# One scores tile for a chunk, weight parts loaded two entries ahead, half the norm products, the sinks' exponential last

## The chip, the cores and the metric

The kernel runs on one core of one Trainium2 chip. It is one launch. The metric is the device time of that launch in microseconds, as the median of several runs. Beside it one execution was taken by the hardware profiler; its views are what the prediction argues from.

## What is computed

One decoder block on 2048 positions of width 1024, all in float32. Cut to the part that the change touches:

```python
q = partial_rope(rmsnorm(q, q_norm), positions) * scale     # 16 query heads of 64
k = partial_rope(rmsnorm(k, k_norm), positions)             # 2 key heads
s = q @ k.T over the block before and the own block, window 128, else -inf
m = maximum(max(s), sink)
p = exp(s - m);  denom = sum(p) + exp(sink - m)
out = (p / denom) @ v
x = x + (sigmoid(gate_pool) * pooled + sigmoid(gate_attn) * out) @ w_out
x = x + (silu(gate) * val) @ w_down                          # after a causal convolution of width 3
```

Ahead of it stand one projection of the normed input into pooling channels, queries, keys, values and two gates, and a pooling mixer with four windows.

## The kernel before

The sequence is worked in two chunks of 1024 positions, one after the other. A chunk runs through the same stages: `mixer` (keys and values, queries, attention, pooling, gates), `out_proj`, `up` and the class `Down`. The change touches `mixer` alone. A product in float32 is made as three products of rounded halves (`mm3`, L235), so every projection of 128 channels by 512 positions (`project`) is 24 matmuls into one PSUM bank. Two such banks exist (tag `f`), two of tag `a`, two of tag `t`, and one double bank of tag `s`.

**Keys stage.** For each of the 8 blocks of 128 positions, `raw` makes 24 matmuls of 256 columns into a bank `a`, `block_a` and `block_b` norm and rotate the keys, and `turn` transposes them (L714). Between the blocks stand fillers: in the first chunk the folding of two weight matrices (`fold`) and the query projections of own = 1; in the second chunk the query projections alone.

**Query projections.** `queries(c, j, n, ...)` projects the 128 channels j of 8 (j // 4 is `own`, a half of the 16 heads) for the half n of the chunk's positions. For the norm of each head the squares of the 4 projections of one `own` are summed over the head's channels. Before, a pair of projections (j even, then j odd) had an accumulator of its own from the pool `qp` (tag `Q`, 6 buffers of 2 KB a partition): ACT squares the even one into it (L736), squares the odd one into a second Q tile (L739), DVE adds the two (L740), and TensorE multiplies the sum with `heads8`, a 0/1 matrix, in 4 matmuls of 8 columns (L753). The trace shows each of these as two records of a matmul and two of a weight load. DVE adds the first pair's result to e1 (L756) and the second pair's to that (L759), and GpSimd raises it to -0.5 (L761). The rotated, split queries go to DRAM (`qd`) and come back one block at a time.

**Attention.** `mixer` walks over 32 items per chunk: 4 groups of 4 heads, 8 blocks each. An item's `scores` makes 8 matmuls of 256 columns (L797; at a chunk's start L799 and L802) into the double bank `s`, of which there is one. DVE masks them (L806), takes the maximum (L811), makes the exponent's bias (L812, L813) and the sinks' exponent (L814). ACT makes the exponential of the sinks (L815) and of the scores, one instruction per head (L818) with the sum over a row, and DVE divides (L820 to L822). `probabilities`, one item later, transposes them (L829), splits them (L831, L832) and masks them on GpSimd (L835); `values`, two items later, multiplies with the values (L854). One or two projections (queries, gates, pooling channels) stand behind each item as fillers.

**Weights.** The class `Stream` hands out weights in a fixed list of entries. When entry i is taken, the loads up to i + 2 are issued and the parts (the rounded halves) up to i + 2 are made. In the first chunk a part is made by ACT and DVE from a loaded tile, and written to DRAM. In the second chunk a part is not made but loaded back from there (`made`, 1 MB each) into one of the 19 buffers of pool `up` (tag `U`), and the load is issued at the time at which the part would have been made.

**Order.** The program is written in one order, and a scheduler puts each engine's instructions into an order of its own when the program is built: an instruction comes when the scheduler takes its inputs and its buffer to be ready. So an edit in one place shifts the order on all engines around it. The engines then work their lists strictly in order, and every load and store stands in the one list of SP.

Of the kernel before, what the change touches and what calls it, by code (L numbers as in the profile page):

```python
# [16 lines left out]
F32 = mybir.dt.float32  # L17
F32R = mybir.dt.float32r
I32 = mybir.dt.int32
U8 = mybir.dt.uint8  # L20
AF = mybir.ActivationFunctionType
ALU = mybir.AluOpType
# [4 lines left out]
P = 128  # L27
# [48 lines left out]
class Stream:  # L76
# [27 lines left out]
            self.loaded += 1  # L104

    def part(self, n):
        while self.parted < min(n, len(self.entries)):
            self.tiles[self.parted] = self.split(self.entries[self.parted],
                                                 self.raws.pop(self.parted))
            self.parted += 1  # L110
# [81 lines left out]
def block_kernel(ctx: ExitStack, tc: tile.TileContext, x, xT, pos, vec, qkn, w_poolT, w_pool, w_q, w_kv,  # L192
                 w_gp, w_ga, w_out, w_up, w_down, outT):
    nc = tc.nc
    V, G, A = nc.vector, nc.gpsimd, nc.scalar
# [6 lines left out]
    up_ = pool("up", 19)  # L202
    fp = pool("fp", 4)
    mp = pool("mp", 5)
    qp = pool("qp", 6)
    sp = pool("sp", 2)
    ps = pool("ps", 2, space=PSUM)
    ps2 = pool("ps2", 1, space=PSUM)
# [19 lines left out]
    between = []  # L228
# [158 lines left out]
    raw = [rp.tile([P, 8, P], F32, "R") for _ in range(3)] + [mp.tile([P, 8, P], F32, "M")]  # L387
# [242 lines left out]
    def project(hs, w, n, tag="f"):  # L630

        c = slice(n * 512, (n + 1) * 512)
        out = ps.tile([P, 512], F32, tag)
        mm3(out, [(w[:, 0, k, :], w[:, 1, k, :], hs[k][:, 0, c], hs[k][:, 1, c])
                  for k in range(KT)])
        if between:
            between.pop()()
        return out, c
# [88 lines left out]
    def queries(c, j, n, hs, ta, st):  # L727
        if n == 0:
            st["q", j] = stream.get("q", j, later=later)
        pq, c_ = project(hs, st["q", j], n)  # L730
        if j % 2 == 0:
            st["raw"] = mp.tile([P, 2, 512], F32, "M"), qp.tile([P, 512], F32, "Q")
        raw, acc = st["raw"]
        A.copy(raw[:, j % 2], pq)
        if j % 2 == 0:
            A.square(acc, pq)  # L736
            return
        sq = qp.tile([P, 512], F32, "Q")
        A.square(sq, pq)  # L739
        V.tensor_add(acc, acc, sq)  # L740
        parts = up_.tile([P, 2, 2, 512], F32R, "U")
        if j % 4 == 1:
            rotate(raw, st["rows"], c_, parts[:, 0].bitcast(F32))
        A.copy(parts[:, 0], raw)
        V.tensor_sub(parts[:, 1], raw, parts[:, 0].bitcast(F32))
        own, at = j // 4, j % 4
        for i in range(2):
            for e, r in enumerate(STARTS[at - 1 + i]):
                load(qd[own][n][:, r:r + 8].rearrange("a d h t -> (d h) a t"),
                     parts[64 * e:64 * e + 64, :, i].bitcast(F32))  # L750
        pn = ps.tile([P, 512], F32, "t")[:, 0:32].rearrange("p (b h) -> p b h", b=4)
        for b in range(4):
            nc.tensor.matmul(pn[:, b], acc[:, b * P:(b + 1) * P], heads8, start=True, stop=True)  # L753
        r = rq[:, own, 4 * n:4 * n + 4]
        if at == 1:
            V.tensor_tensor(r, pn, e1[:, c, 4 * n:4 * n + 4].unsqueeze(2)  # L756
                            .to_broadcast([P, 4, 8]), op=ALU.add)
        else:
            V.tensor_add(r, pn, r)  # L759
            r = r.rearrange("p b h -> p (b h)")  # L760
            G.tensor_tensor(r, r, mhalf, op=ALU.pow)  # L761

    def rotate(x, rows, c_, t):

# [20 lines left out]
    def scores(it):  # L785
        c, q4, n, g, qT = it["c"], it["q4"], it["n"], it["q4"] // 2, it["qT"]
        b = c * NB + n
        kt = it["kts"][g]
        sc = ps2.tile([P, 4, 256], F32, "s")
        if b == 0:  # L790
            V.memset(sc[:, :, 0:P], -1e30)
        for h in range(4):
            st = qT[:, h, :]
            for a in range(2):
                fl = dict(start=(a == 0), stop=(a == 1))
                if n > 0:
                    nc.tensor.matmul(sc[:, h, :], st, kt[:, a, (n - 1) * P:(n + 1) * P], **fl)  # L797
                else:
                    nc.tensor.matmul(sc[:, h, P:256], st, kt[:, a, 0:P], **fl)  # L799
            if n == 0 and b > 0:  # L800
                for a in range(2):
                    nc.tensor.matmul(sc[:, h, 0:P], st, it["carry"][:, a], start=(a == 0),  # L802
                                     stop=(a == 1))


        V.copy_predicated(sc[:, :, 0:P], causal.unsqueeze(1).to_broadcast([P, 4, P]),  # L806
                          sc[:, :, P:256])
        sk = slice(4 * q4, 4 * q4 + 4)
        st = sp.tile([P, 6, 4], F32, "st")
        mx, nm, es, rs, dn = (st[:, i] for i in range(5))  # L810
        V.reduce_max(mx, sc[:, :, 0:P], axis=AX.X)  # L811
        V.scalar_tensor_tensor(nm, mx, -1.0, it["rq"], op0=ALU.mult, op1=ALU.mult)  # L812
        V.tensor_tensor(nm, nm, nsink[:, sk], op=ALU.min)  # L813
        V.tensor_sub(es, nm, nsink[:, sk])  # L814
        A.activation(es, es, AF.Exp)  # L815
        pr = qp.tile([P, 4, P], F32, "Q")
        for h in range(4):
            A.activation(pr[:, h, :], sc[:, h, 0:P], AF.Exp, bias=nm[:, h:h + 1],  # L818
                         scale=it["rq"][:, h:h + 1], accum_out=rs[:, h:h + 1])
        V.tensor_add(dn, rs, es)  # L820
        V.reciprocal(dn, dn)
        V.tensor_tensor(pr, pr, dn.unsqueeze(2).to_broadcast([P, 4, P]), op=ALU.mult)  # L822
        it["pr"] = pr
# [554 lines left out]
    def mixer(c, hs, kvw):  # L1378
        kts, vs, raw, block_a, block_b, turn = keys_values(c, hs, kvw)
        ta, st = {}, {}  # L1380
        if c > 0:
            st["rows"] = rope_rows(c)
        for n in range(NB):
            if c == 0 and n == 2:
                st["rows"] = rope_rows(c)
            if c == 0 and n == 0:
                load_rest()
            if c == 0 and n == 1:
                make_h(0, 1, hs)
            if c == 0 and n == 3:  # L1390
                make_h(0, 2, hs)
                for i in range(4, NB):
                    squares(0, i, row(0, i))
            pk = [raw(0), raw(1)] if n == 0 else pk[1:] + ([raw(n + 1)] if n + 1 < NB else [])
            fills = list(first_fillers(c)[n])
            if c == 0 and n == 0:
                for i in range(4):
                    squares(0, i, rows[i])
            if c == 0 and n % 4 == 0:
                norm1(0, n, n + 4)  # L1400
                spread(r1[:, 0, n:n + 4], n * P)
            block_a(n, pk[0])
            block_b(n)
            if n == 2 and c == 0:
                turn(0)
            for f in fills:
                filler(*f, c, hs, ta, st)
            if n > 1 or n == c == 1:
                turn(n - 1)
            run_later()  # L1410
        turn(NB - 1)
        keep_weights(("kv",), kvw)
        items = [dict(c=c, q4=q4, n=n, kts=kts, vs=vs, ta=ta)
                 for q4 in (3, 2, 1, 0) for n in range(NB)]
        for it in items[0:2]:
            load_queries(it)
        for i in range(len(items)):
            group, n = divmod(i, NB)
            scores(items[i])
            if i + 2 < len(items):  # L1420
                load_queries(items[i + 2])
            if i > 1:
                values(items[i - 2])
            run_later()
            fills = fillers(c, group)[n]
            if i > 0 and len(fills) == 1:
# [24 lines left out]
        return ms + [mixed(ta, 0)]  # L1451
# [89 lines left out]
```

## Time and profile before

| | us |
|---|---|
| median of 3 runs | 2463.49 |
| lowest and highest of them | 2461.58, 2464.21 |
| the profiled execution | 2459.19 |
| span in its trace | 2456.9 |
| TensorE busy in the span | 2421.4 |
| VectorE (DVE), ScalarE (ACT) busy | 1876.9, 1124.8 |

The profiled execution's own time is 2.3 us longer than the span of its trace, and 4.3 us below the median. In the views PE stands for TensorE's matmuls, PEld for its weight loads, SP for the queue of the transfers. "L753 PE MATMUL t<-heads,Q" is a matmul of source line 753 into a tile of tag t from the tiles heads8 and Q. In a view of idle time "<- DVE Q L740" names the instruction whose end let the engine go on. In the view of waits the numbers are the microseconds in total, how often, and the longest. The first chunk's mixer stage ends at about 520 us, the second chunk's runs from 1240 to about 1730 us.

### The profile page before, as it was taken

What the parts mean: (1) busy time and instruction counts of PE and PEld (TensorE: products, weight loads), DVE (VectorE), ACT (ScalarE), POOL (GpSimd) and SP (SyncE); (2) the same over time, 40 slices, a digit from 0 to 9 for tenths busy, and PEclk for the clock granted to TensorE, in tenths of its full rate; (3) what the DMA queues carried; (4) which work ended last, traced back from release to release, by engine and by line L of the source; (5) the groups of instructions that cost most, each with busy time, mean ns of one, the idle gap of its engine ahead of it and who ended that gap; (6) DMA issues with size and microseconds to landing.
All of it is one profiled execution on the core that took longest, in us unless ns stands there. A gap on an engine that the chain in (4) does not pass through costs nothing.

```text
span 2456.9 us, 30720 instructions
## 1 busy us (share of the span) xinstructions
PE 2421.4 (99%) x11398; PEld 2010.8 (82%) x11398; DVE 1876.9 (76%) x3028; ACT 1124.8 (46%) x2150; POOL 146.5 (6%) x101
## 2 busy tenths in 40 slices
PE   9999999999999999999999999999999999999999
PEld 8877888887888888788888788888888888887887
DVE  8687887766988878899845767665569888788994
ACT  7445444444555555543522433333445554554432
POOL 0113111100000000000002211110000000000000
PEclk9999999999999999999999999999999999999999
DMA  9664452368222233644333542131553222228321
GB/s 338 224 197 133 172 180 110 109 220 296 97 77 86 94 112 108 211 164 143 132 125 124 166 146 100 57 125 48 184 172 103 77 87 90 82 69 283 131 75 52
DMA packets 139029, 337.88 MB, mean 138 GB/s; under 512 B 12288, under 2 KB 48640, under 8 KB 127872
## 3 DMA queue, kind: packets, MB, share of 16 engines
q1 hardware_dynamic: 138880, 335.92, 40.1%
q8 instruction: 90, 1.47, 0.2%
q14 instruction: 59, 0.48, 0.1%
HBM read 231.67 MB, written 104.20 MB: 137 GB/s over the span
## 4 chain that ended last, share of the span: by engine, by line
PE 87%; DVE 8%; ACT 2%; DMA 1%; issue 1%; POOL 0%; SPq 0%; DVEq 0%; ACTq 0%; POOLq 0%
PE f L235 31%; PE f L1069 18%; PE t L1069 10%; PE a L1069 4%; PE a L1359 4%; PE f L1359 4%; PE s L1359 4%; PE t L1359 4%; PE s L797 2%; PE a L854 2%; PE a L235 2%; DVE F L906 1%; ACT Q L818 1%; PE t L829 1%; PE t L753 1%
## 5 line engine op out<-in xcount | busy, mean ns | idle before, releaser
L235 PE MATMUL f<-U,U 128*128 128x512 f32 (+1 forms) x3936 | 918.8, 389 | 7.9 <-DVE U L219 3.7
L235 PEld LDWEIGHTS f<-U,U 128*128 128x128 f32 x3936 | 725.4, 188 | 158.3 <-DVE U L219 7.2
L1069 PE MATMUL f<-U,U 128*128 128x512 f32 x1512 | 359.7, 389 | 1.3 <-ACT Q L1087 1.3
L1069 PEld LDWEIGHTS f<-U,U 128*128 128x128 f32 x1512 | 283.3, 188 | 61.6 <-ACT Q L1087 2.2
L1135 DVE SCALAR_TENSOR_TENSOR M<-F,vc,M 128x1024 f32<-128x1024 f32 x176 | 225.0, 1282 | 127.9 <-ACT M L1132 127.5
L1069 PE MATMUL t<-U,U 128*128 128x512 f32 x1080 | 254.5, 389 | 0.3 <-ACT Q L1087 0.3
L1069 PEld LDWEIGHTS t<-U,U 128*128 128x128 f32 x1080 | 202.5, 188 | 43.2 <-ACT Q L1087 1.1
L818 ACT ACTIVATE Q<-s,st,rq 128x128 f32<-128x128 f32 x256 | 114.2, 453 | 139.6 <-DVE st L813 123.4
L331 ACT CAST U<-R 128x1024 fp32r<-128x1024 f32 x120 | 125.4, 1053 | 65.7 <-DVE R L352 34.0
L332 DVE TENSOR_TENSOR U<-R,U 128x1024 fp32r<-128x1024 f32 x120 | 146.7, 1222 | 0.0
L1069 PE MATMUL a<-U,U 128*128 128x512 f32 x576 | 138.6, 389 | 0.0
L1069 PEld LDWEIGHTS a<-U,U 128*128 128x128 f32 x576 | 108.0, 188 | 22.3
L1069 PE MATMUL f<-U,M 128*128 128x512 f32 x504 | 122.3, 390 | 4.0 <-DVE F L1113 4.0
L1318 ACT CAST U<-U 128x1024 fp32r<-128x1024 f32 x74 | 77.0, 1050 | 87.3 <-PE a L1359 26.8
L835 POOL TENSOR_SCALAR_AFFINE_SELECT M<-M 128x1024 fp32r<-128x1024 f32 x64 | 81.8, 1279 | 579.0 <-DVE M L832 331.4
L1069 PEld LDWEIGHTS f<-U,M 128*128 128x128 f32 x504 | 94.4, 188 | 24.4 <-DVE F L1113 4.9
L1132 ACT ACTIVATE M<-F,vc 128x1024 f32<-128x1024 f32 x88 | 109.3, 1243 | 1.3
L1121 ACT COPY F<-f 128x512 f32<-128x512 f32 x42 | 24.7, 587 | 178.3 <-PE f L1069 178.3
L219 DVE TENSOR_TENSOR U<-R,U 128x512 fp32r<-128x512 f32 x142 | 93.6, 691 | 7.2 <-ACT U L218 5.9
L1319 DVE TENSOR_TENSOR U<-U,U 128x1024 fp32r<-128x1024 f32 x74 | 89.7, 1221 | 11.0 <-ACT U L1318 11.0
L218 ACT CAST U<-R 128x512 fp32r<-128x512 f32 x142 | 80.6, 617 | 20.4 <-DMA R<-w_ga 5.1
L1318 ACT CAST F<-U 128x1024 fp32r<-128x1024 f32 x46 | 48.3, 1050 | 88.2 <-PE a L1359 52.3
(269 smaller groups left out, 3669.2 us busy)
## 6 DMA issues: line engine op xcount, KB each, us to landing
R<-w_up SPq DMA_DIRECT2D x80, 512.0 KB, 3.7
actd<-M SPq DMA_DIRECT2D x44, 512.0 KB, 2.6
U<-w_down SPq DMA_DIRECT2D x88, 256.0 KB, 5.3
U<-actd SPq DMA_DIRECT2D x88, 256.0 KB, 5.4
qd<-U SPq DMA_DIRECT2D x64, 256.0 KB, 3.7
Q<-qd SPq DMA_DIRECT2D x64, 256.0 KB, 3.8
R<-w_out SPq DMA_DIRECT2D x32, 512.0 KB, 5.1
U<-kept SPq DMA_DIRECT2D x12, 1024.0 KB, 7.5
```

The source lines that it names most:

```text
L219: last = V.tensor_sub(lo[:, t], src[:, t], hi[:, t].bitcast(F32))
L235: nc.tensor.matmul(out, a, b, start=(i == 0), stop=(i == n - 1))
L331: A.copy(t[:, 0], raw)
L332: V.tensor_sub(t[:, 1], raw, t[:, 0].bitcast(F32))
L818: A.activation(pr[:, h, :], sc[:, h, 0:P], AF.Exp, bias=nm[:, h:h + 1], scale=it["rq"][:, h:h + 1], accum_out=rs[:, h:h + 1])
L835: G.affine_select(own.rearrange("p a h q -> p (a h) q"), pa.bitcast(F32).rearrange("p a h q -> p (a h) q"), pattern=[[0, 8], [1, P]], base ...
L1069: nc.tensor.matmul(bank, a[:, x, k, :], b[k // 2][:, y, k % 2, :], start=(first and i == 0), stop=(i == 11), skip_group_check=True)
L1132: A.activation(y, u[:, 2:], AF.Identity, bias=cw[:, 3, m:m + 1], scale=cw[:, 2, m:m + 1])
L1135: V.scalar_tensor_tensor(y, u[:, j:j + T], cw[:, j, m:m + 1], y, op0=ALU.mult, op1=ALU.add)
L1318: A.copy(hi, src)
L1319: V.tensor_sub(lo, src, hi.bitcast(F32))
L1359: nc.tensor.matmul(into[m], u[:, 0, c_], v[:, 1], start=(first and j == 0), stop=(k == n - 1 and j == 2), skip_group_check=True)
```

## The change

It has four parts, all within `mixer` and the weight stream.

1. The double bank `s` is taken once for all 32 items of a chunk, where each item took it anew.
2. Where the entry taken last but one is a gate or a pooling weight and the part to come is one that lies in DRAM already (second chunk), its load is issued one entry earlier.
3. The squares of all 4 projections of an `own` go into one accumulator, so 4 matmuls with `heads8` per `own` and half remain of 8, and one addition per pair more is made on DVE (3 additions of 128x512 where there were 2). The squares go into tiles that exist already (the raw tile's second half, or the parts' tile) in place of a Q tile. The matmuls stand in the list `between`, from which the next projection takes them behind its own 24.
4. In `scores` the sinks' exponent and exponential (L814, L815) are written behind the four exponentials of the scores.

```diff
     def part(self, n):
+        if self.used > 0 and self.entries[self.used - 1][0] in ("ga", "pu", "pg"):
+            n += n in self.raws and self.raws[n] is None
         while self.parted < min(n, len(self.entries)):
...
+        own, at = j // 4, j % 4
+        if at == 0:
+            st["acc", n] = qp.tile([P, 512], F32, "Q")
+        acc = st["acc", n]
         if j % 2 == 0:
-            st["raw"] = mp.tile([P, 2, 512], F32, "M"), qp.tile([P, 512], F32, "Q")
-        raw, acc = st["raw"]
+            st["raw"] = mp.tile([P, 2, 512], F32, "M")
+        raw = st["raw"]
         A.copy(raw[:, j % 2], pq)
-        if j % 2 == 0:
+        if at == 0:
             A.square(acc, pq)
             return
-        sq = qp.tile([P, 512], F32, "Q")
+        if at == 2:
+            A.square(raw[:, 1], pq)
+            V.tensor_add(acc, acc, raw[:, 1])
+            return
+        parts = up_.tile([P, 2, 2, 512], F32R, "U")
+        sq = parts[:, 1, 0].bitcast(F32)
         A.square(sq, pq)
         V.tensor_add(acc, acc, sq)
-        parts = up_.tile([P, 2, 2, 512], F32R, "U")
...
+        if at == 3:
+            between.append(lambda: query_norms(c, own, n, acc))
+
+    def query_norms(c, own, n, acc):
         pn = ps.tile([P, 512], F32, "t")[:, 0:32].rearrange("p (b h) -> p b h", b=4)
         for b in range(4):
             nc.tensor.matmul(pn[:, b], acc[:, b * P:(b + 1) * P], heads8, start=True, stop=True)
...
-        sc = ps2.tile([P, 4, 256], F32, "s")
+        if n == 0 and q4 == 3:
+            it["bank"]["s"] = ps2.tile([P, 4, 256], F32, "s")
+        sc = it["bank"]["s"]
...
-        V.tensor_sub(es, nm, nsink[:, sk])
-        A.activation(es, es, AF.Exp)
         pr = qp.tile([P, 4, P], F32, "Q")
         for h in range(4):
             A.activation(pr[:, h, :], sc[:, h, 0:P], AF.Exp, bias=nm[:, h:h + 1],
                          scale=it["rq"][:, h:h + 1], accum_out=rs[:, h:h + 1])
+        V.tensor_sub(es, nm, nsink[:, sk])
+        A.activation(es, es, AF.Exp)
```

What it moves is seen in the built programs; lines of the changed kernel have numbers that are 3 to 15 higher (`mm3` is L238, the norm matmul L768, the transposition of keys L717, the exponentials L831 and L834, the splits of weights L222).

On TensorE, in the keys stage of the second chunk, before: the end of a key block (bank a_10656) with the norm matmuls of a query pair in it, and the next projection's begin (f_10707).

```order
L235 MATMUL a_10656<-U_10419,U_10309 128x256 x3
L235 MATMUL a_10656<-U_10419,U_10326 128x256 x3
L753 MATMUL t_10641<-heads_6_179,Q_10543 128x8 x4
L714 MATMUL t_10647<-identr_91,Q_10512 128x128 x4
L235 MATMUL a_10656<-U_10419,U_10345 128x256 x3
L235 MATMUL a_10656<-U_10419,U_10364 128x256 x3
L235 MATMUL f_10707<-U_10219,U_10421 128x512 x3
```

The same stage in the changed program, at the first norm matmuls that it has there: the last of the 24 matmuls of one projection (f_11007), and the next one (f_11076).

```order
L238 MATMUL f_11007<-U_10282,U_10584 128x512 x3
L238 MATMUL f_11007<-U_10301,U_10584 128x512 x3
L768 MATMUL t_11032<-heads_6_179,Q_10479 128x8 x4
L717 MATMUL t_11043<-identr_91,Q_10907 128x128 x4
L238 MATMUL f_11076<-U_10156,U_10859 128x512 x3
```

The norm matmuls of the first pair are gone, those that remain stand behind a whole projection that follows the one whose squares they sum, and there are 8 groups of them in the program where there were 16.

On ScalarE, at an item of the first chunk, before: the exponentials of the scores (L818, s_3414) with that of the sinks (L815) among them.

```order
L929 ACTIVATE F_3306<-f_3387,vc_145 128x512
L818 ACTIVATE Q_3430,st_3424<-s_3414,st_3424,rq_229 128x128 x2
L815 ACTIVATE st_3424<-st_3424 128x4
L818 ACTIVATE Q_3430,st_3424<-s_3414,st_3424,rq_229 128x128 x2
L864 COPY Q_3445<-a_3440 64x256
```

And in the changed program, at an item of the same group.

```order
L846 CAST M_3904<-t_3899 128x512
L831 ACTIVATE Q_3867,st_3863<-s_1598,st_3863,rq_229 128x128 x4
L834 ACTIVATE st_3863<-st_3863 128x4
L879 COPY Q_3884<-a_3879 64x256 x2
L900 ACTIVATE F_3913<-f_3914,vc_145 128x512
```

Before, the sinks' exponential stood within the four exponentials in 63 of the 64 items; now it stands behind them in all.

On VectorE, in the keys stage of the first chunk, before: the split of a fold's weights (L219, into U_898 and M_903) and the rotation and squares of the second query projection (L769, L770, L740).

```order
L770 SCALAR_TENSOR_TENSOR M_830<-M_830,vc_145,U_688 64x512
L219 TENSOR_TENSOR U_898<-R_794,U_898 128x512 x2
L219 TENSOR_TENSOR M_903<-R_796,M_903 128x256 x2
L691 TENSOR_TENSOR Q_969<-vf_218 128x2x64
L769 SCALAR_TENSOR_TENSOR U_872<-M_830,vc_145,U_688 64x512
L740 TENSOR_TENSOR Q_831<-Q_831,Q_869 128x512
```

And in the changed program, the rotation (L781 to L784), the addition of the squares (L752) and the same split (L222, U_891).

```order
L781 SCALAR_TENSOR_TENSOR U_869<-M_831,vc_145,U_688 64x512
L752 TENSOR_TENSOR Q_830<-Q_830,U_869 128x512
L782 SCALAR_TENSOR_TENSOR M_831<-M_831,vc_145,U_688 64x512
L783 TENSOR_TENSOR M_831<-M_831,U_869 64x512
L784 TENSOR_TENSOR M_831<-M_831,U_869 64x512
L222 TENSOR_TENSOR U_891<-R_794,U_891 128x512 x2
```

The split of the fold's weights has moved from ahead of the second projection's rotation to behind it.

More of the change, by code (lines that the diff above doesn't have):

```diff
@@ L730, in queries @@
         pq, c_ = project(hs, st["q", j], n)
+        own, at = j // 4, j % 4
+        if at == 0:
+            st["acc", n] = qp.tile([P, 512], F32, "Q")
+        acc = st["acc", n]
         if j % 2 == 0:
-            st["raw"] = mp.tile([P, 2, 512], F32, "M"), qp.tile([P, 512], F32, "Q")
-        raw, acc = st["raw"]
+            st["raw"] = mp.tile([P, 2, 512], F32, "M")
+        raw = st["raw"]
         A.copy(raw[:, j % 2], pq)
-        if j % 2 == 0:
+        if at == 0:
             A.square(acc, pq)
             return
-        sq = qp.tile([P, 512], F32, "Q")
+        if at == 2:
[4 more added lines that the diff above has]
+        sq = parts[:, 1, 0].bitcast(F32)
         A.square(sq, pq)
         V.tensor_add(acc, acc, sq)
-        parts = up_.tile([P, 2, 2, 512], F32R, "U")
-        if j % 4 == 1:
+        if at == 1:
             rotate(raw, st["rows"], c_, parts[:, 0].bitcast(F32))
@@ L745, in queries @@
         V.tensor_sub(parts[:, 1], raw, parts[:, 0].bitcast(F32))
-        own, at = j // 4, j % 4
         for i in range(2):
@@ L754, in queries @@
         r = rq[:, own, 4 * n:4 * n + 4]
[L755 to L761, printed above, removed]
+        V.tensor_tensor(r, pn, e1[:, c, 4 * n:4 * n + 4].unsqueeze(2).to_broadcast([P, 4, 8]),
+                        op=ALU.add)
+        r = r.rearrange("p b h -> p (b h)")
+        G.tensor_tensor(r, r, mhalf, op=ALU.pow)
     def rotate(x, rows, c_, t):
@@ L1412, in mixer @@
         keep_weights(("kv",), kvw)
-        items = [dict(c=c, q4=q4, n=n, kts=kts, vs=vs, ta=ta)
+        bank = {}
+        items = [dict(c=c, q4=q4, n=n, kts=kts, vs=vs, ta=ta, bank=bank)
                  for q4 in (3, 2, 1, 0) for n in range(NB)]
```

## The prediction

> **What bounds the kernel.** I read the page first: its span, and its first part, the busy time of each engine.
>
> ```profile
> span 2456.9 us, 30720 instructions
> PE 2421.4 (99%) x11398; PEld 2010.8 (82%) x11398; DVE 1876.9 (76%) x3028; ACT 1124.8 (46%) x2150; POOL 146.5 (6%) x101
> ```
>
> TensorE is busy for 2421.4 of 2456.9 us. Only two things can shorten this kernel: fewer or cheaper matmuls, or less of the 35.5 us in which TensorE is idle. So the second view is that of the waits of TensorE: who waits, on whom, the total in us, how often, the longest. Of its list I show the rows in which an instruction stands that the change touches or that lies in the same stage.
>
> ```profile
> PE s L797 <- ACT Q L818: 9.7, 16, 1.8
> PE f L235 <- DVE U L219: 3.7, 5, 0.9
> PE t L753 <- DVE Q L740: 2.6, 4, 1.0
> PE f L235 <- ACT Q L736: 0.8, 1, 0.8
> ```
>
> The score matmuls wait longest, for the exponentials that read the one bank `s`; the norm matmuls wait in four places for the addition of squares. In no row of the list does TensorE wait for the transfer of a weight part in the second chunk.
>
> **The norm matmuls, 8 groups for 16.** The groups of instructions give their busy time, and the chain of waits (start, us, what, here of the second chunk's keys stage and first items) shows how long the chain stands on one of them before it goes on.
>
> ```profile
> L753 PE MATMUL t<-heads,Q 128*128 128x8 f32 x128 | 16.5, 255 | 2.6 <-DVE Q L740 2.6
> 1306.96 0.93 PE t L753 x8
> 1307.90 0.37 PE t L714 x4
> 1353.51 0.88 PE t L753 x8
> 1354.39 0.49 PE t L829 x4
> 1402.96 1.06 PE t L753 x8
> 1404.02 3.51 PE f L235 x15
> ```
>
> There are 128 records, 8 to a group, so 16 groups, on average 16.5 / 16 = 1.03 us each. The mean of one record (255 ns) is no price, since records overlap. What a group takes from the chain is the distance from its start to the next piece: 0.94, 0.88 and 1.06 us here. I take 0.98, nearly the middle of 0.88 and 1.06; 8 groups that go are 7.8 us (7.0 to 8.5). All of it is on the path, because TensorE has no slack in these stages.
>
> The Trainium skill, page "TensorE: Matmul & The Clock Gate", Part 1 on the clock gate, says that the distance of two matmuls never falls below about 25 ns however few columns they have, and by that a group of 8 records would be 0.2 us and the 8 groups 1.6 us. The rows above do not agree with that price: by them a record of 8 columns takes 0.88 / 8 = 0.11 us or more.
>
> **The waits in front of them.** Two of the four, from the timeline of TensorE (in brackets the idle time before, and its releaser):
>
> ```profile
> 212.38 1.03 PE L753 MATMUL t<-heads,Q 128*128 128x8 f32 x8 [0.87 <-DVE Q L740]
> 1415.45 1.03 PE L753 MATMUL t<-heads,Q 128*128 128x8 f32 x8 [1.04 <-DVE Q L740]
> 1376.13 5.51 PE f L235 x24
> ```
>
> Before, a group followed close behind the projection whose squares it sums, and met the addition. Now each of the 8 stands behind one further projection, and the last row (chain of waits) prices that: 5.51 us. The longest wait was 1.04 us, so nothing is left of it: −2.6. The bound is −1.3, half, in case the projections that follow meet their own bank sooner instead (the wait of L235 on L736 above is such a one). Who reads the norms is not hurried: GpSimd's power and the first scores with them come a stage later.
>
> **The sinks' exponential behind the others.** The timeline of ScalarE at one item (start, us, operation), and, for the instruction L815, what its engine waited for ahead of it.
>
> ```profile
> 347.53 0.45 ACT L818 ACTIVATE Q<-s,st,rq 128x128 f32<-128x128 f32 x1
> 347.96 0.20 ACT L815 ACTIVATE st<-st 128x4 f32<-128x4 f32 x1
> 348.06 0.46 ACT L818 ACTIVATE Q<-s,st,rq 128x128 f32<-128x128 f32 x1
>   DVE st L814: 4.3, 8
> ```
>
> Exponentials of scores follow each other in 0.43 us (347.53 to 347.96), and the sinks' pushes the fourth by 0.10 us (to 348.06). In the 16 waits of L797 that is 1.6 us. Eight times ScalarE also stood 4.3 us in all for the exponent L814 ahead of it, but how many of these eight fall on the 16 items with a wait no row says. I take 0.4 of the 4.3, near its small share: 2.0 in all, with bounds 0.8 (half of the 1.6) and 5.9 (1.6 + 4.3).
>
> **One scores tile.** Its gain could be that a head's score matmul waits only for that head's exponential.
>
> ```profile
> 1366.14 1.21 PE L797 MATMUL s<-U,Q 128*128 128x256 f32 x8 [1.85 <-ACT Q L818]
> ```
>
> This, the longest of the waits, holds up the whole group of 8 matmuls. In the built program of the change the first score matmul of an item still stands behind the fourth exponential of the item before, as it did, and the other seven behind it. The sole bank is the same bank. I take 0; the gain if I misread it is a rival.
>
> **Weight parts two entries ahead.** A transfer that nobody waits for gains nothing by an earlier start: 0. It costs a buffer of `up` earlier, which the previous parts have left by then; were that false, the load would queue ahead of others in SP's list.
>
> **What is added.** Two rows of the groups of VectorE (count, total, mean ns, idle time before), its load in two stretches (busy us behind those of TensorE and its weight loads), and the place of the fold:
>
> ```profile
> L740 DVE TENSOR_TENSOR Q<-Q,Q 128x512 f32<-128x512 f32 x16 | 11.0, 685 | 22.2 <-ACT Q L739 21.9
> L219 DVE TENSOR_TENSOR U<-R,U 128x512 fp32r<-128x512 f32 x142 | 93.6, 691 | 7.2 <-ACT U L218 5.9 <-DMA U<-xT 0.8
> 142.00:220.00 78.00, 74.17 (x378) 60.38 (x378) 62.65 (x129) 42.65 (x124) 21.67 (x10) 1.00 0.51 157
> 1333.00:1420.00 87.00, 82.44 (x424) 67.86 (x423) 65.32 (x130) 36.96 (x112) 16.89 (x9) 0.98 0.42 134
> 62.73 0.74 DVE L769 SCALAR_TENSOR_TENSOR U<-M,vc,U 64x512 f32<-64x512 f32 x1 [1.84 <-ACT M L734]
> 63.40 0.68 DVE L740 TENSOR_TENSOR Q<-Q,Q 128x512 f32<-128x512 f32 x1
> 64.00 0.74 DVE L770 SCALAR_TENSOR_TENSOR M<-M,vc,U 64x512 f32<-64x512 f32 x1
> 64.67 0.67 DVE L771 TENSOR_TENSOR M<-M,U 64x512 f32<-64x512 f32 x1
> 65.27 0.68 DVE L772 TENSOR_TENSOR M<-M,U 64x512 f32<-64x512 f32 x1
> 64.13 1.06 PE L753 MATMUL t<-heads,Q 128*128 128x8 f32 x8
> 65.40 3.11 PE L235 MATMUL f<-M,U 128*128 128x256 f32 x24
> ```
>
> There are 24 additions for 16: 8 × 0.685 = 5.5 us more on VectorE. It is busy for 62.65 of 78 us and 65.32 of 87 where the additions lie, so idle time covers them; what waits behind one is at worst a split of weights or a mask of scores. TensorE had 3.7 us of waits on such splits, so the cover is not whole: bounds 0 and 5.5, and I take 0.5, near the small end, since those 3.7 us come from 142 splits.
>
> The fold's matmuls began at 65.40. Their weights' split now stands behind the second rotation: VectorE would start it at 65.27 + 0.60 = 65.9 (the steps here follow in 0.60), two steps of 0.60 and the last's tail end it at 67.2. TensorE, less a norm group (0.94), is there at 64.5. So 0 to 2.8 us are new, 0 if another matmul stands between. I take 1.0.
>
> **The sum.** −7.8 − 2.6 − 2.0 + 1.0 + 0.5 = −10.9 us. The profiled execution took 2459.19, so 2448.3; the median of before is 2463.49, so **2452.6**. With all bounds on the good side (−8.5 − 2.6 − 5.9) it is −17.0, 2446.5; on the bad (−7.0 − 1.3 − 0.8 + 2.8 + 0.5) −5.8, 2457.7. From no change a measurement can tell about 0.2%, 4.9 us here.
>
> **Rivals.**
>
> *The scores are freed head by head.* Then the whole 9.7 us of L797 goes in place of the 2.0: −18.6, 2444.9. For it: it is the largest wait, and the tile is what changes. Against it: the order of the built program, above.
>
> *The new work eats it.* The eight additions lie on the path in full (5.5) and the fold waits 2.8: −10.9 − 1.5 + 8.3 = −4.1, 2459.4, within 0.2%. For it: VectorE is at 80% and 75% in the two stretches. Against it: it idles 22.2 us ahead of the additions that exist, for ScalarE's squares.
>
> *A norm matmul costs only its columns.* The 5.51 us for 24 matmuls of 512 columns are 0.23 us each, so 8 columns 0.0036, and 64 records 0.23 us: the removal brings 0.2 in place of 7.8, −3.3, 2460.2, within 0.2%. Against it: the distances of 0.88 to 1.06 in the chain, unless they hide what would have been idle time.
>
> By the Trainium skill's 25 ns a matmul (same page and part as above) this case would be an estimated 1.6 in place of 7.8, 2458.8.
>
> *Slower: the Q buffers run out.* Two accumulators now live through the keys stage and the first eight items of a chunk, and hold two of six Q buffers; before, one lived for a pair of projections only. Queries, probabilities and output copies share the four that are left. What a late start of a query load costs is bounded by its time to land, the last number of these rows of DMA issues (two stretches, at each chunk's first items):
>
> ```profile
> Q<-qd SPq DMA_DIRECT2D x8, 256.0 KB, 5.0
> Q<-qd SPq DMA_DIRECT2D x8, 256.0 KB, 4.5
> ```
>
> If the score matmuls of these 16 items each wait as long as the longest wait of before, 1.85, that adds 29.6: +18.7, 2482.2. It decides from 10.9 / 16 = 0.68 us an item, and is slower by 0.2% from (10.9 + 4.9) / 16 = 0.99. For it: 4 buffers, and a load that takes 5.0 us. Against it: the loads stand two items ahead, and a projection of 5.51 us stands behind each item, about one load's landing.
>
> That the change doesn't do what it says: the load two entries ahead and the one tile are such cases, both at 0 in the sum.
>
> **Chances.** The forecast 0.70; scores freed 0.06; gain eaten 0.13; only columns 0.04; buffers run out 0.07. The forecast and the first rival are faster by over 0.2% (below 2458.6): 0.76. The second and third are within: 0.17. Slower: 0.07. The forecast's own range, 2446.5 to 2457.7, rests on bounds that may be off at both ends, so I give it 0.6 of its 0.70; with the three small rivals, down to 2444.9 and up to 2460.2, the range 2444.5 to 2460.5 holds 0.83.
>
> **What would show it.** Right: 64 records of norm matmuls in 8 groups, no wait on the addition of squares; ScalarE's four exponentials without a gap of 0.10; waits of the score matmuls near 7.7 of 9.7 us; TensorE busy about 8 us less. A wait of the fold's matmuls near 65 us on the split of weights shows the new cost. Wrong: score matmuls that wait for a query's load in the first eight items of a chunk; score waits near 0; TensorE's busy time unchanged; or new waits for the splits of 5 us and more.

## The result, and the profile after

The changed kernel takes **2440.23 us** (median of 4 runs, 2439.09 to 2443.05), the kernel before beside it 2462.69 us (4 runs, 2461.58 to 2464.21). The ratio is 0.991, with a 95% interval of 0.9893 to 0.9927: 22.5 us faster, twice the 10.9 us that were forecast, and below the range. The profiled executions differ by 2459.19 − 2439.09 = 20.1 us, their spans by 19.8 us; before's lay 3.5 us under its median, after's 1.1 us under.

The page of the changed kernel, its span and busy times:

```profile
span 2437.1 us, 30604 instructions
PE 2409.8 (99%) x11334; PEld 2004.0 (82%) x11334; DVE 1883.0 (77%) x3028; ACT 1123.9 (46%) x2150; POOL 147.1 (6%) x101
```

TensorE is busy for 11.6 us less and idle for 8.2 us less (35.5 before, 27.3 now). VectorE works 6.1 us more (1876.9 before), near the 5.5 us priced for the eight additions. The waits of TensorE: two lines that answer to those shown of before, and three that before's list does not have (L869, L238 on L221, L844):

```profile
PE s L812 <- ACT Q L831: 4.4, 12, 0.6
PE f L238 <- DVE U L222: 4.1, 6, 0.9
PE a L869 <- POOL M L850: 1.6, 2, 1.3
PE f L238 <- ACT U L221: 1.1, 2, 0.7
PE t L844 <- DVE Q L837: 0.8, 1, 0.8
```

The score matmuls (L812, exponentials L831) wait 4.4 us, not 9.7. No norm matmul waits. The three new waits come to 3.5 us. The wait of the value matmuls on ScalarE's split of probabilities, which stood in before's list and which the prediction did not quote, is gone; its row there, and those of both attention stages, in us, TensorE's busy time and the other engines', before and then after:

```profile
PE a L854 <- ACT M L831: 2.2, 3, 0.7
131.40:557.90 426.50, 419.26 (x2028) 346.98 (x2026) 325.90 (x647) 201.40 (x536) 53.18 (x34) 1.00 0.46 161
1334.50:1665.20 330.70, 322.38 (x1605) 268.24 (x1604) 225.36 (x465) 128.37 (x410) 48.08 (x32) 0.99 0.33 112
```

```profile
130.50:551.50 421.00, 416.37 (x2011) 345.38 (x2010) 328.40 (x646) 200.71 (x536) 54.10 (x34) 1.00 0.47 163
1324.40:1646.00 321.60, 318.39 (x1596) 266.69 (x1596) 227.75 (x468) 127.61 (x410) 48.01 (x32) 1.00 0.35 115
```

The stages run from the first score matmul of a chunk to the same point after attention. The first is 5.5 us shorter, the second 9.1 us; of the second's, 5.1 us are idle time (8.3 before, 3.2 now), more than the 1.7 us that the norm matmuls waited there. Its granted clock (third number from the end) rose from 0.99 to 1.00.

Over the whole span the clock is the same: both profiled executions have a mean of 0.999. Before lost about 1.6 us between 1390 and 1430 us (40 us at 0.96), the changed kernel as much in its first 40 us (0.96, where before has 1.00). So the 19.8 us between the two spans hold no clock: 8.2 are idle time, 7.6 the norm groups (worked out below), and for the other 4.0 of TensorE's busy time no row was found.

### The profile page after: what moved, and what is told of

It is laid out like the page before. It is cut to its first block, busy times and chain, and to the rows that moved or that the text cites. A ratio compares the mean times of both kernels' runs of the same rounds, so it can differ in the third digit from the quotient of the medians.

```text
span 2437.1 us, 30604 instructions
## 1 busy us (share of the span) xinstructions
PE 2409.8 (99%) x11334; PEld 2004.0 (82%) x11334; DVE 1883.0 (77%) x3028; ACT 1123.9 (46%) x2150; POOL 147.1 (6%) x101
## 4 chain that ended last, share of the span: by engine, by line
PE 88%; DVE 7%; ACT 2%; DMA 1%; issue 1%; SPq 0%; POOL 0%; DVEq 0%; ACTq 0%; POOLq 0%
PE f L238 32%; PE f L1084 18%; PE t L1084 9%; PE a L1084 4%; PE a L1374 4%; PE f L1374 4%; PE s L1374 4%; PE t L1374 4%; PE s L812 2%; PE a L869 2%; PE a L238 2%; DVE F L921 1%; ACT Q L831 1%; PE t L844 1%; DVE U L1040 1%
## 5 line engine op out<-in xcount | busy, mean ns | idle before, releaser
L238 PE MATMUL f<-U,U 128*128 128x512 f32 (+1 forms) x3936 | 919.2, 390 | 7.7 <-DVE U L222 4.1
L238 PEld LDWEIGHTS f<-U,U 128*128 128x128 f32 x3936 | 726.7, 188 | 158.2 <-DVE U L222 7.3
L831 ACT ACTIVATE Q<-s,st,rq 128x128 f32<-128x128 f32 x256 | 113.8, 454 | 145.6 <-DVE st L828 136.0
L222 DVE TENSOR_TENSOR U<-R,U 128x512 fp32r<-128x512 f32 x142 | 93.8, 693 | 7.6 <-ACT U L221 7.3
L221 ACT CAST U<-R 128x512 fp32r<-128x512 f32 x142 | 80.5, 618 | 16.4 <-DMA R<-w_ga 9.5
```

The lines of the kernel that those rows point to most:

```text
L222: last = V.tensor_sub(lo[:, t], src[:, t], hi[:, t].bitcast(F32))
L238: nc.tensor.matmul(out, a, b, start=(i == 0), stop=(i == n - 1))
```

## The experiments

Twelve kernels were run, each timed beside the kernel before. "Clock" is the mean granted clock over all runs of a kernel, each given to 0.001; for before it was 0.9973 over 50 runs, and 0.001 of it is 2.4 us of the span. The medians of before, in the third column, lie between 2461.29 and 2462.78, so a difference of 1.5 us or less between two kernels that were timed beside different ones says nothing.

| kernel | median us (runs) | before | ratio, 95% interval | clock |
|---|---|---|---|---|
| the changed kernel | 2440.23 (4) | 2462.69 | 0.9910, 0.9893 to 0.9927 | 0.9985 |
| no_tile | 2440.00 (4) | 2461.66 | 0.9907, 0.9891 to 0.9922 | 0.9988 |
| no_ahead | 2444.41 (5) | 2461.66 | 0.9928, 0.9915 to 0.9940 | 0.9978 |
| no_norm | 2456.46 (9) | 2461.66 | 0.9975, 0.9965 to 0.9985 | 0.9973 |
| no_sinks | 2445.21 (5) | 2461.66 | 0.9927, 0.9914 to 0.9939 | 0.9988 |
| norm_x3 | 2458.72 (11) | 2461.29 | 0.9986, 0.9977 to 0.9995 | 0.9973 |
| norm_now | 2446.01 (5) | 2461.29 | 0.9937, 0.9924 to 0.9949 | 0.9982 |
| only_ahead | 2459.62 (11) | 2461.29 | 0.9996, 0.9987 to 1.0005 | 0.9969 |
| only_sinks | 2457.97 (11) | 2461.29 | 0.9989, 0.9980 to 0.9998 | 0.9975 |
| pairs_late | 2448.38 (5) | 2462.78 | 0.9940, 0.9928 to 0.9953 | 0.9978 |
| sub_first | 2440.02 (4) | 2462.78 | 0.9908, 0.9893 to 0.9923 | 0.9988 |
| norm_r | 2437.03 (4) | 2462.78 | 0.9892, 0.9878 to 0.9905 | 0.9988 |
| dense_x | 2453.26 (6) | 2462.78 | 0.9966, 0.9953 to 0.9979 | 0.9987 |

### Each part undone by itself

**no_tile**:

```diff
-        if n == 0 and q4 == 3:
-            it["bank"]["s"] = ps2.tile([P, 4, 256], F32, "s")
-        sc = it["bank"]["s"]
+        sc = ps2.tile([P, 4, 256], F32, "s")
```

> The changed kernel, but each item takes the double bank s anew as before. Theory A (the gain is the norm matmuls with their waits, and the sinks' exponential): one tile is worth nothing, so about 2440 (2438 to 2442), score waits near 4.4 us in total. Theory B (one tile frees the score matmuls or moves their place in the built order, and that is the part of the gain that the forecast lacks): the 5 us that the score waits lost come back, with what follows them: 2446 or more, score waits near 9.

2440.00 us, and score waits of 4.5 us. The one scores tile is worth nothing; theory B falls.

**no_ahead**:

```diff
-        if self.used > 0 and self.entries[self.used - 1][0] in ("ga", "pu", "pg"):
-            n += n in self.raws and self.raws[n] is None
```

> The changed kernel, but weight parts of the second chunk are loaded at the old time. Theory A: nobody waits for these transfers, 2440 (2438 to 2442). Theory C (the earlier loads take transfers out of the way of the query loads, which lets items start earlier and gives the missing 10 us): 2447 or more, with the difference in the second chunk's mixer stage alone.

2444.41 us, 4.2 more. Its interval overlaps that of the changed kernel, but its lowest run (2443.63) is above the highest of the 12 runs of the changed kernel, no_tile and sub_first, which time alike (2443.21). So theory A's zero falls, and theory C's place is right: the second attention stage. But its mechanism is not: the wait that came back is not on a query or a transfer. Its row in the list of no_ahead, and TensorE's timeline at one of the three places:

```profile
PE a L866 <- ACT M L843: 2.2, 3, 0.7
1436.16 0.60 PE L841 MATMUL t<-identr,Q 128*128 128x128 f32 x4
1437.49 0.50 PE L866 MATMUL a<-M,U 128*128 128x512 f32 x1 [0.73 <-ACT M L843]
1437.83 4.51 PE L235 MATMUL f<-U,U 128*128 128x512 f32 x19
```

and the same item in the changed kernel:

```profile
1432.77 1.09 PE L869 MATMUL a<-M,U 128*128 128x512 f32 x4
1433.70 5.61 PE L238 MATMUL f<-U,U 128*128 128x512 f32 x24
1439.15 0.60 PE L844 MATMUL t<-identr,Q 128*128 128x128 f32 x4
```

In no_ahead a value matmul stands directly behind the transposition (L841) whose result ScalarE has yet to split for it, and ahead of the projection. The built order has it so:

```
L841 MATMUL t_12227<-identr_91,Q_12097 128x128 x4
L866 MATMUL a_12288<-M_12232,U_10362 128x512
L235 MATMUL f_12201<-U_10156,U_12121 128x512 x3
```

Of the four matmuls of that value product the first is pulled ahead of the projection, whose part (U_12121) is a loaded one. With the load an entry earlier the scheduler puts the projection first. A load that nobody on the chip waited for had still set the order.

These waits are 2.2 of the 4.2 us. The clock of 0.9978, for 0.9985, is another 1.7; the slow stretches of no_ahead's trace (0.96 from 540 to 580 us, 0.95 from 1005 to 1040) lie ahead of the stage that the loads touch, so that the loads cause them is not shown.

**no_norm**: the old norm products in the changed kernel (16 groups, one accumulator a pair, close behind their own projection). The code for it is that of before; of the edit only the place of the matmuls is shown.

```diff
-        if at == 3:
-            between.append(lambda: query_norms(c, own, n, acc))
+        for b in range(4):
+            nc.tensor.matmul(pn[:, b], acc[:, b * P:(b + 1) * P], heads8, start=True, stop=True)
```

> The changed kernel with the old norm products (16 groups, an accumulator for each pair, right behind their projection). Theory A: the 8 groups cost 8.9 us of busy time and their waits 2.6: 2440 + 11.5 = 2451.5 (2449 to 2454). Theories B and C, with the forecast's price of 7.8 and waits that other work takes over: 2448 (2446 to 2449).

2456.46 us, 16.2 more, above all theories' figures; this is the part that brings most. Its waits for the addition are there again:

```profile
PE t L756 <- DVE Q L743: 3.4, 5, 1.0
PE s L803 <- ACT Q L822: 5.5, 9, 1.5
```

**no_sinks**: L814 and L815 of before ahead of the four exponentials.

```diff
+        V.tensor_sub(es, nm, nsink[:, sk])
+        A.activation(es, es, AF.Exp)
         pr = qp.tile([P, 4, P], F32, "Q")
...
-        V.tensor_sub(es, nm, nsink[:, sk])
-        A.activation(es, es, AF.Exp)
```

> The changed kernel, but the sinks' exponent and exponential are written ahead of the scores' exponentials as before. Theory A: most of the 5 us that the score waits lost come from here: 2444 to 2446, score waits 8 to 9 us. Theory B: only the 2.0 us of the forecast, 2442, score waits near 6.

2445.21 us, 5.0 more, though the intervals overlap and its runs reach from 2439.45 to 2446.86. Its score waits are 5.7 us, 1.3 above the changed kernel's. The means of the runs, 2444.05 and 2440.65, differ by 3.4 us, near the 3.3 us of only_sinks below. The time is theory A's, the wait is theory B's, and what makes up the difference was not found in a row.

The four undone parts sum to 16.2 + 4.2 + 5.0 − 0.2 = 25.2 us, against 22.5 together.

### The norm groups: number, place, price

**norm_x3**:

```diff
-        for b in range(4):
+        for b in [0, 1, 2, 3] * 3:
             nc.tensor.matmul(pn[:, b], acc[:, b * P:(b + 1) * P], heads8, start=True, stop=True)
```

> The changed kernel with each of its 8 groups of norm matmuls issued three times over (the same products again), so 16 groups more in the same places, without a wait in front. Theory A1 (a group costs what the chain of before showed, 0.98 us): 2440.2 + 15.7 = 2456. Theory A2 (a group costs its busy share, 1.1 us or more, because its neighbours start later too): 2458 or more. Theory D (a group standing behind a projection is much cheaper, and the 12 us of its removal were waits): below 2450.

2458.72 us: 18.5 more for 16 groups, 1.16 each, theory A2. But the timeline shows groups of 2.60 / 3 = 0.87 us (from the start of the 24 records to the next row):

```profile
1406.38 2.74 PE L768 MATMUL t<-heads,Q 128*128 128x8 f32 x24
1408.98 0.64 PE L844 MATMUL t<-identr,Q 128*128 128x128 f32 x4
```

In all eight places together these steps are 20.7 us, and 6.6 us in the changed kernel: 14.1 of the 18.5 us. A2's reason, neighbours that start later, was not found; of the rest the clock holds about 3 us (0.9985 to 0.9973), see dense_x, and for 1.5 us no row was found.

**norm_now**:

```diff
-            between.append(lambda: query_norms(c, own, n, acc))
+            query_norms(c, own, n, acc)
```

> The changed kernel with its 8 norm groups asked for at once, not behind one further projection; the scheduler then puts them some 15 matmuls after their own projection. If the place carries a good part of the gain: 3 us of waits for the addition of squares come back, and 2443 to 2445. If the number of groups carries it all: 2440 to 2442.

2446.01 us, 5.8 more, beyond the upper figure of 2445. Its waits for the addition, from the view of waits, the longest of them in the timeline with the row behind it, and the same group in the changed kernel:

```profile
PE t L768 <- DVE Q L752: 2.3, 3, 1.1
1406.97 1.03 PE L768 MATMUL t<-heads,Q 128*128 128x8 f32 x8 [1.09 <-DVE Q L752]
1407.86 0.31 PE L814 MATMUL s<-U,Q 128*128 128x128 f32 x1
```

```profile
1404.31 5.72 PE L238 MATMUL f<-U,U 128*128 128x512 f32 x24
1409.87 0.95 PE L768 MATMUL t<-heads,Q 128*128 128x8 f32 x8
1410.67 1.21 PE L812 MATMUL s<-U,Q 128*128 128x256 f32 x8
```

Close behind its projection the group takes 0.89 us after the wait, behind a further one 0.80. So the place is worth the wait, 2.3 us, and about 0.09 us a group more, 0.7; the remaining 2.8 of the 5.8 us stand in no list of waits. The clock (0.9982 for 0.9985) is 0.7 of them.

**pairs_late**, the fourth corner: 16 groups, each behind a further projection. Again the code is that of before, and of the edit only the place of the matmuls is shown.

```diff
-        pn = ps.tile([P, 512], F32, "t")[:, 0:32].rearrange("p (b h) -> p b h", b=4)
+        between.append(lambda: query_norms(c, own, at, n, acc))
+
+    def query_norms(c, own, at, n, acc):
+        pn = ps.tile([P, 512], F32, "t")[:, 0:32].rearrange("p (b h) -> p b h", b=4)
```

> The changed kernel with 16 norm groups as before (an accumulator for each pair), but each behind one further projection, as the change has its 8. With no_norm (16 groups, close behind their own projection), norm_now (8, close) and the changed kernel (8, behind a further one) this is the fourth corner. If number and place add up: 8 groups at the price that norm_x3 gave (1.1 us) above the changed kernel, 2449. If the place carries most: 2445 or less. If the number carries all: 2454 or more.

2448.38 us: 8.2 above the changed kernel, 8.1 below no_norm. Number and place add up, and each carries half of the 16.2.

**dense_x**, for what the groups cost beyond their time:

```diff
+        for _ in range(more):
+            nc.tensor.matmul(out, pairs[0][0], pairs[0][2], start=True, stop=True)
...
-        pq, c_ = project(hs, st["q", j], n)
+        pq, c_ = project(hs, st["q", j], n, more=8 if j % 4 == 3 else 0)
```

> The changed kernel with 64 more matmuls of 512 columns, 8 ahead of each fourth projection (each writes what the first of the 24 then overwrites): 64 x 0.228 = 14.6 us more work for TensorE, as much as the 16 groups of 8 columns of norm_x3, but dense. Theory G (norm groups and short waits also cost granted clock, since TensorE counts as little used in them): 2440.2 + 14.6 = 2454.8, with the granted clock of the changed kernel, 0.9985 on average. Rival (the clock goes by time or by chance): as norm_x3, 2458.5 and 0.9973.

2453.26 us, 13.0 more (by the mean of its runs 2454.75, 14.1 above the changed kernel's mean of 2440.65), with a clock of 0.9987; norm_x3 lost 18.5 at 0.9973. Ten microseconds of the second chunk, at the last norm groups, in before, norm_x3, dense_x and the changed kernel (us, TensorE's busy time, granted clock):

```profile
1410.00:1420.00 10.00, 8.96 (x49) 0.86 0.35 111
```

```profile
1410.00:1420.00 10.00, 10.00 (x49) 0.83 0.36 131
```

```profile
1410.00:1420.00 10.00, 10.00 (x55) 1.00 0.36 122
```

```profile
1410.00:1420.00 10.00, 10.00 (x56) 1.00 0.50 163
```

In norm_x3 TensorE was not idle at all here; it had just passed 24 records of 8 columns, and ran ten microseconds at 0.83, which is 1.7 us lost. It lost as much from 110 to 120 us (0.83), behind its first tripled group at 110.52. Dense work of the same length did that nowhere in the attention stages.

Only one execution of a kernel has rows, but the kernels can be laid side by side. The 40 us around the second chunk's last norm groups, in no_norm, pairs_late, norm_now and the changed kernel, two groups in each:

```profile
1390.00:1430.00 40.00, 37.60 (x189) 0.96 0.50 158
1390.00:1430.00 40.00, 38.65 (x201) 1.00 0.51 163
1390.00:1430.00 40.00, 38.53 (x191) 0.96 0.51 162
1390.00:1430.00 40.00, 40.00 (x209) 1.00 0.61 203
```

The clock there is 0.96 in all six kernels whose groups stand close behind their projection or are tripled (before, no_norm, only_ahead, only_sinks, norm_now, norm_x3), and 1.00 in the eight others. So theory G holds for groups in a long row and for groups with a wait right in front, and not for single groups behind a further projection, which pairs_late has too, with 1.35 us of idle time in the same 40 us. Not every loss is of this kind: no_ahead loses the clock from 540 to 580 us, where there is no norm group.

The Trainium skill, page "TensorE: Matmul & The Clock Gate", section "What's actually happening", has the array at half rate after an idle window of about 3.4 us, until a busy window follows; for one window that is an estimated 1.7 us. The slices agree with the size (10 × 0.17), but not with idleness as the only cause: in norm_x3 TensorE was busy for 10.00 of the 10.00 us from 1400 to 1410, ahead of the loss.

**norm_r**, an attempt at a better kernel: the sum of squares is rounded to the form fp32r, for which the trace shows one record a matmul where it showed two.

```diff
+        if at == 3:
+            accr = qp.tile([P, 512], F32R, "Q")
-        V.tensor_add(acc, acc, sq)
+        V.tensor_add(accr if at == 3 else acc, acc, sq)
...
-            nc.tensor.matmul(pn[:, b], acc[:, b * P:(b + 1) * P], heads8, start=True, stop=True)
+            nc.tensor.matmul(pn[:, b], acc[:, b * P:(b + 1) * P], heads8r, start=True, stop=True)
```

> The changed kernel, with the sum of squares rounded to the form that TensorE takes in one pass, in a Q tile of its own (the norms lose digits by that), so that a norm group is 4 matmuls and 4 weight loads of one pass. If the passes make the price of a group: 8 groups at a quarter to a half of 0.9 us, 2434.5 to 2437. If its price is fixed per matmul: 2438 to 2440. Against it: a sixth Q tile is asked for at that moment, which could make queries or probabilities wait, 2442 or more.

2437.03 us, 3.2 less than the changed kernel (intervals overlap). A group now steps 0.36 us for 0.80:

```profile
1407.35 0.50 PE L772 MATMUL t<-heads8r,Q 128*128 128x8 f32 x4
1407.71 1.21 PE L816 MATMUL s<-U,Q 128*128 128x256 f32 x8
```

8 × 0.44 = 3.5 us, the median's 3.2. The price goes with the number of matmul records and their weight loads (4 for 8), at 0.09 to 0.10 us each.

### The other parts alone on the kernel before

**only_ahead**:

```diff
+        if self.used > 0 and self.entries[self.used - 1][0] in ("ga", "pu", "pg"):
+            n += n in self.raws and self.raws[n] is None
```

> The kernel before with nothing changed but the loads of the second chunk's weight parts. Theory E (the early load changes no transfer that anybody waited for, but the order that the scheduler writes: three times a value matmul no longer stands between the transposition of its own probabilities and a projection): the three waits of 0.73 us on the split of probabilities go, 2462 - 2.2 = 2460 or, with the clock that a wait costs, 2458. The forecast's 0: 2462, three waits still there.

2459.62 us, 1.7 less than before; the interval of the ratio, 0.9987 to 1.0005, holds no change and theory E's 2460. The three waits on the split of probabilities are gone from its list, so the mechanism is there; its size on this base stays inside the noise.

**only_sinks**:

```diff
-        V.tensor_sub(es, nm, nsink[:, sk])
-        A.activation(es, es, AF.Exp)
...
+        V.tensor_sub(es, nm, nsink[:, sk])
+        A.activation(es, es, AF.Exp)
```

> The kernel before with nothing changed but the sinks' exponent and exponential behind the scores'. By the forecast's 2.0 us: 2460. By the undoing in the changed kernel (about 4): 2458, with the score waits at 5 us in place of 9.7.

2457.97 us, 3.3 less than before, and score waits of

```profile
PE s L797 <- ACT Q L816: 5.6, 8, 1.8
```

in place of 9.7 in 16: half the waits went whole. The timelines of before say which; ScalarE and then TensorE at two items:

```profile
186.15 0.21 ACT L815 ACTIVATE st<-st 128x4 f32<-128x4 f32 x1 [0.68 <-DVE st L814]
186.26 0.44 ACT L818 ACTIVATE Q<-s,st,rq 128x128 f32<-128x128 f32 x1
186.84 0.39 PE L797 MATMUL s<-U,Q 128*128 128x256 f32 x1 [0.77 <-ACT Q L818]
1389.43 0.20 ACT L815 ACTIVATE st<-st 128x4 f32<-128x4 f32 x1 [0.67 <-DVE st L814]
1389.55 0.44 ACT L818 ACTIVATE Q<-s,st,rq 128x128 f32<-128x128 f32 x1
1390.13 1.10 PE L797 MATMUL s<-U,Q 128*128 128x256 f32 x7 [0.49 <-ACT Q L818]
```

ScalarE stood 0.68 us for the exponent (L814) with one exponential still to come, and the score matmuls of the next item waited 0.77 us for that exponential. Seven of the eight waits of L815 in before are followed by a wait of L797 in this way, 3.1 us of the 9.7. In only_sinks these seven are gone, and the eight waits that stay all stand at items where ScalarE had not waited for the exponent. Taking at each of the seven the smaller of the two waits, ScalarE's standing can have cost 2.7 us.

**sub_first**, to part the two instructions:

```diff
+        V.tensor_sub(es, nm, nsink[:, sk])
         pr = qp.tile([P, 4, P], F32, "Q")
...
-        V.tensor_sub(es, nm, nsink[:, sk])
         A.activation(es, es, AF.Exp)
```

> The changed kernel, with the sinks' exponent again ahead of the exponentials on VectorE, and its exponential still the last on ScalarE. Theory F (the cost of before was ScalarE standing, with exponentials still to come, for an exponent that VectorE had not made, and the 0.10 us of the step itself): all of the gain stays, 2440 (2438 to 2442). Rival (the exponent's place on VectorE made the gain): half of it or more goes, 2442.5 or more.

2440.02 us: all of the gain stays. ScalarE's order makes it, not VectorE's. Theory F holds.

## Why the prediction was wrong

The direction was right, the size half of it. By the prediction's own steps:

- **Norm matmuls, −7.8, and their waits, −2.6: right for TensorE's own time.** The 16 groups of before step 0.81 to 0.92 us each in the timeline, 14.2 us in all, the 8 of after 6.6; that is −7.6. The 0.98 a group, read off the chain, was too much for before (0.89), and the groups that stay became cheaper. The waits of 2.6 went.
- **Missing from that step: the clock.** The prediction read the granted clock of the two stretches and used it nowhere. The mean granted clock over all runs rose from 0.9973 to 0.9985; of a span of 2450 us that is 2.9 us, and 2.7 us is what the medians differ more than the two profiled spans, whose clocks are equal. That groups in a long row lower it, norm_x3 beside dense_x shows; that groups close behind their projection do too, the 40 us of no_norm and pairs_late show (0.96 and 1.00). How much of the 2.9 us is theirs is not shown, since the clock is lost in other places as well. This is a term that the sum lacked, and half of why no_norm loses 16.2 and not 10.4; some 3 us of the 16.2 remain beside it. The 0.9985 rests on 4 runs; no_tile and sub_first, which time alike, have 0.9988.
- **Sinks' exponential, −2.0: mis-sized.** The step that failed says that no row tells how many of the eight waits for L814 fall on items with a wait, and takes 0.4 of the 4.3 us. The two timelines, laid beside each other, tell it: seven of eight, up to 2.7 us. By the runs the term is 3 to 5 (only_sinks 3.3, no_sinks 5.0 by medians and 3.4 by means).
- **Weight parts two entries ahead, 0: wrong.** "A transfer that nobody waits for gains nothing" looked only for waits on the chip. The scheduler orders TensorE by its own idea of when a part lands, and an earlier load put projections ahead of value matmuls at the three places: 2.2 us of waits, 4.2 us by no_ahead, of which 1.7 go with its lower clock. The row of the 2.2 us was in the list, and the moved rows in the built order.
- **One scores tile, 0: right** (no_tile).
- **New work, +1.5: not where it was looked for.** The fold's weights came about a microsecond later than the forecast 67.2, but other matmuls stood between, the case that the step had priced at 0. VectorE's split and, of TensorE, the fold's first 4, then the rest:

```profile
67.03 1.28 DVE L222 TENSOR_TENSOR U<-R,U 128x512 fp32r<-128x512 f32 x2
65.58 0.64 PE L238 MATMUL f<-M,U 128*128 128x256 f32 x4
66.07 0.45 PE L717 MATMUL t<-identr,Q 128*128 128x128 f32 x4
66.36 1.43 PE L238 MATMUL a<-U,U 128*128 128x256 f32 x10
67.76 2.68 PE L238 MATMUL f<-M,U 128*128 128x256 f32 x20
```

Ahead of the first score matmul TensorE waits 7.0 us in before and 7.0 us after, so the keys stage of the first chunk lost nothing by waits. But three waits are new, 3.5 us in all: the value matmuls on GpSimd's mask (L869, 1.6), projections and folds on ScalarE's splits (L221, 1.1, of which 0.7 in the fold at 74 us) and a transposition (L844, 0.8). The first is in every kernel that has one accumulator for four projections (1.6 to 1.9 us), 0.6 us in pairs_late and not in no_norm, so it belongs to the norm part; what causes the other two was not tested.

Taken together, 7.6 for the groups, 2.6 for their waits, 3.3 to 5.0 for the sinks, 2.2 for the loads and 2.9 for the clock are 18.6 to 20.3 of the 22.5 us, before the new waits are taken off. The bad end of the forecast's range also held a slip: it took 0.5 us for the additions, whose own bound was 5.5, and would have been 2462.7 with it; the measured time lies beyond the other end.

The rivals: scores freed head by head fell (no_tile, and score waits of 4.4 us, not 0). "Only its columns", and with it the 25 ns of the Trainium skill's page as a price, fell: a record steps 0.09 to 0.10 us. Buffers did not run out (in no row of the list does a score matmul wait for a query's load), and the new work did not eat the gain.

What stays open: at least 2.2 of the 22.5 us; the time of no_sinks (5.0 us by medians, 3.4 by means), of which its rows show 1.3 us of score waits; and about 2 us of what the close place of the groups costs in norm_now.

## What to carry to other kernels

Where one engine is busy 99% of the time, every part of a change that a scheduler orders is to be looked up in the built order at the places where that engine waits, a load's time among them: a load that no engine waits for can still set who stands first. When a wait has two possible sources, the timelines of both engines, laid side by side, say how many of the waits belong to each. A run of small matmuls costs its own time, and a long one, or one right behind a wait, may lower the clock of what comes behind it, 1.7 us a time here.

## What was not expected of the hardware

A row of 24 records with 8 columns each was followed by a lower granted clock of TensorE with no idle time in it (norm_x3: 0.83 over 10 us, in two of its eight places), while as much time in matmuls of 512 columns was not (dense_x: 0.9987 on average, norm_x3 0.9973). A single group of 8 records was followed by the loss only where it stood close behind its projection (0.96 over 40 us in no_norm, 1.00 in pairs_late). And the same group costs 0.80 us behind a further projection and 0.89 close behind its own, in five of the eight places of norm_now without any wait in front of it; why is not shown.
